# An encoder step on one core: the first attention block's query preparation moved ahead of the last gates, into shared ring buffers

## The chip, the cores and the metric

The kernel runs on one core of a Trainium2 chip. The metric is device time in microseconds (us) of one execution. Engines are named as the profile names them: PE (TensorE matmuls) with PEld (its weight loads), DVE (VectorE), ACT (ScalarE), POOL (GpSimd) and SP (SyncE, whose queue issues the DMAs).

## The reference, cut to what matters

One layer of a streaming encoder for 1024 prompt tokens and 64 sample tokens, width 1024, all in float32. One projection of the normalised input gives the columns of three branches and three gate blocks:

```
h = rmsnorm(x)
qa, ka, va, qi, ki, wi, ub, qm, gates = split(h @ w_in)
a = top-k sparse attention (8 query heads, 2 kv heads, head_dim 64)
b = causal pooling mixer of ub
m = cross-attention (4 heads, head_dim 128) into 256 memory tokens
mixed = sigmoid(ga)*(a @ w_oa) + sigmoid(gb)*(b @ w_ob) + sigmoid(gm)*(m @ w_om)
x = x + mixed @ w_out;  x = x + SwiGLU(rmsnorm(x))
```

Here only the gates `ga`, the memory branch `m`, its output product with `w_om` and the start of the attention branch `a` matter.

## The kernel before, in words

Every float32 product is made of three passes on halves: a value is split into a rounded high part and a low remainder, and `matmul3` (L117 to L124) issues high times high, high times low and low times high. A split costs one copy on ACT or POOL (`round_hi`) and one subtraction on DVE (`lo_of`, L88).

The code is written in one order, and a planner orders each engine's instructions when the program is built: an instruction that stands earlier in the code goes first among those that are ready, and one that stands later may be put into the gaps. What is fixed then is each engine's list; on the chip every engine works through its list in order and waits at each entry for its semaphores. `tc.issue_after(x)` puts the instructions of its block behind `x` in the list of `x`'s engine. A tile is a piece of a pool; tiles with one tag share the few buffers of this tag (`bufs`), each new tile taking a buffer that an older one has given back.

The part of the program that matters, in code order:

- The projections of the attention's queries, keys and values, nine token blocks each (L560 to L625). A key block is normalised, rotated, split (`kd`, L592 and L593), transposed on PE (L599), copied (`kt`, L602) and stored (`k_t`, L603).
- Gate blocks as fillers: `fill_gate(8, ...)` and `fill_gate(16, ...)`, then `fill_ob()`, the pooling branch's output product.
- The memory branch (L717 to L853), two halves of two heads each, in each half eight blocks of 128 tokens in a pipeline: queries transposed (L761), split (`qh`, `ql`), six logit products, softmax (maximum on DVE L727, exponential on ACT L732, scaling on POOL L735), transposes of the probabilities (L741), split (`ph`, `pl`), and for each pair of blocks twelve products with the values (L806, which the profile shows as L124 `mm<-ph,vh` and its like). Its result is split into `bh`, `bl`. Beside the blocks each half computes the 64 sample tokens (`sample`). The branch's key and value tiles are of tag `raw` (3 buffers): in each half `kc`, `vc`, and in step 1 of `sample` another `kc`, `vc` and the copy `kct` (L817).
- `fill_gate(0, side_a[:, 0], 0, 8)` (L857): the eight gate blocks of branch a. A block f loads its weights into `fraw`, splits them into one buffer of tag `whi` (POOL, L98) and one of `wlo` (DVE, L88), both tags with 2 buffers, and makes three chunks of 24 products each (`fl<-hh,whi` and its like), 576 products in all; ACT takes a tanh of each chunk (L247), SP stores it (L635). Code order puts them behind the memory branch; in time they fill its gaps.
- One `fill_om` (the memory branch's output product, 12 products), the load of the attention's first keys `kT`, then the first attention block's queries: `q0` (tag `raw`) is loaded (L877), split into `qs0` (L870 on ACT, L871 on DVE), transposed in eight pieces (L883) and copied to `qT0` (L884). `qs0` and `qT0` are tiles of a small pool `early` that lies on memory of the memory branch.
- The attention over query blocks. Its PSUM pool takes the banks of the pool before, and its SBUF pool takes the memory of the normalised input and of the gate tiles. Three `fill_om` come first, then the first block's logits (L1053); `split_values` (L1014, L1015) halves the values between the first softmax and the second.

Of the kernel before, what the change touches and what calls it, by code (L numbers as in the profile page):

```python
# [17 lines left out]
KT = D // 128  # L18
# [29 lines left out]
def encoder_step(ctx: ExitStack, tc: tile.TileContext, a: dict, o: list):  # L48
# [69 lines left out]
    def matmul3(ps, pairs, low_last=False):  # L118
        prods = [[(lh, rh), (lh, rl), (ll, rh)] for lh, ll, rh, rl in pairs]
        if low_last:  # L120
            prods = [[q for p in prods for q in p[:2]], [p[2] for p in prods]]
        prods = [q for p in prods for q in p]
        for i, (l, r) in enumerate(prods):
            PE.matmul(ps, l, r, start=i == 0, stop=i == len(prods) - 1)  # L124

    def rstd(r, ss, inv):
        G.tensor_scalar(r, ss, inv, EPS, op0=OP.mult, op1=OP.add)
# [81 lines left out]
    def raw_tile():  # L209
        return wp.tile([128, 1024], F32, name="raw", tag="raw", bufs=3)  # L210
# [32 lines left out]
    def fsig(w, c0, cn, low_last=False):  # L243
        ps = fps(cn)
        gate_block(w, hh[:, :, c0:c0 + cn], hl[:, :, c0:c0 + cn], ps, low_last)
        sg = fil.tile([128, 384], F32, name="fsg", tag="fsg", bufs=FSG + FPT)[:, :cn]
        A.activation(sg, ps, AF.Tanh, scale=0.5)  # L247
        return sg
# [379 lines left out]

    def fill_gate(base, dst, f0=0, f1=KT):
        for f in range(f0, f1):
            w = fgate(base + f)
            for c0, cn in CH:
                SP.dma_start(dst[f, :, c0:c0 + cn], fsig(w, c0, cn))  # L635

    def prepared(i):
        ts = split_tiles()
# [76 lines left out]
    fill_ob()  # L715

    MS = 128 ** -0.5  # L717
    if True:
        moh, mol = bh, bl
        gp_c = tc.tile_pool(name="gp", bufs=1)  # L720
        gp = gp_c.__enter__()
        with tc.tile_pool(name="matw", bufs=1) as mp:
# [41 lines left out]
            for half in range(2):  # L764
                hs2 = slice(2 * half, 2 * half + 2)
                pt, vc = mem_tiles(mem_k, mem_v, half)
                kh = mp.tile([128, 512], F32R, name="kh", tag="kh", bufs=1)
                kl = mp.tile([128, 512], F32R, name="kl", tag="kl", bufs=1)
                A.copy(kh, pt)
                lo_of(kl, pt, kh)  # L770
                vh = mp.tile([128, 2, 256], F32R, name="vh", tag="vh", bufs=1)
                vl = mp.tile([128, 2, 256], F32R, name="vl", tag="vl", bufs=1)
                A.copy(vh, vc)
                lo_of(vl, vc, vh)
                def query_of(t):
                    ps = queries(t * 128, 128, half)
                    qh = mp.tile([128, 256], F32R, name="qh", tag="qh", bufs=2)
                    ql = mp.tile([128, 256], F32R, name="ql", tag="ql", bufs=2)
                    A.activation(qh, ps, AF.Copy, scale=gqm_c)
                    V.scalar_tensor_tensor(ql, ps, gqm_c, qh.bitcast(F32), op0=OP.mult, op1=OP.subtract)  # L780
                    return qh, ql

                def probs_of(qh, ql):
                    lg = mm()
                    for h in range(2):
                        hs = slice(h * 128, (h + 1) * 128)
                        ms = slice(h * 256, (h + 1) * 256)
                        matmul3(lg[:, ms], [(qh[:, hs], ql[:, hs], kh[:, ms], kl[:, ms])])
                    return mem_softmax(lg, 128)

                def values_of(t, ex, pp_):
                    i = t % 2
                    if i == 0:
                        pp_[:] = [mp.tile([128, 4, 256], F32R, name="ph", tag="ph", bufs=1),
                                  mp.tile([128, 4, 256], F32R, name="pl", tag="pl", bufs=1)]
                    ph, pl = pp_
                    js = slice(i * 128, (i + 1) * 128)
                    pt = probs_t(ex, 128)
                    A.copy(ph[:, :, js], pt)
                    lo_of(pl[:, :, js], pt, ph[:, :, js])  # L800
                    if i == 0:
                        return
                    ps = mm()
                    for h in range(2):
                        hs = slice(h * 128, (h + 1) * 128)
                        matmul3(ps[:, h * 256:(h + 1) * 256],  # L806
                                [(vh[:, i, hs], vl[:, i, hs], ph[:, h * 2 + i], pl[:, h * 2 + i]) for i in range(2)])
                    pv = ps.rearrange("p (h t) -> p h t", h=2)
                    ts = slice((t - 1) * 128, (t + 1) * 128)
                    A.copy(moh[:, hs2, ts], pv)  # L810
                    lo_of(mol[:, hs2, ts], pv, moh[:, hs2, ts])

                def sample(t):
                    if t == 1:
                        pt, vc = mem_tiles(a["cache_mem_k"], a["cache_mem_v"], half)
                        kct = raw_tile()[:, :512]
                        A.copy(kct, pt)  # L817
                        sm_[:] = [vc, kct]
                    if t == 2:
                        ps = queries(SEQ, 64, half)  # L820
                        qs = mp.tile([128, 128], F32, name="qss", tag="qss", bufs=1)
                        A.activation(qs, ps, AF.Copy, scale=gqm_c)
                        sm_.append(qs)
                    if t == 4:
                        lg = mm()
                        for h in range(2):
                            PE.matmul(lg[:64, h * 256:(h + 1) * 256], sm_[2][:, h * 64:(h + 1) * 64],
                                      sm_[1][:, h * 256:(h + 1) * 256], start=True, stop=True)
                        sm_.append(mem_softmax(lg, 64))
                    if t == 6:  # L830
                        pt = probs_t(sm_[3], 64)
                        pT = mp.tile([128, 256], F32, name="pTs", tag="qn", bufs=2).rearrange("p (j t) -> p j t", j=4)
                        A.copy(pT, pt)
                        sm_.append(pT)
                    if t == 7:
                        ps = mm()[:, :128]
                        for h in range(2):
                            for i in range(2):
                                PE.matmul(ps[:, h * 64:(h + 1) * 64], sm_[0][:, i, h * 128:(h + 1) * 128],
                                          sm_[4][:, h * 2 + i], start=i == 0, stop=i == 1)  # L840
                        pv = ps.rearrange("p (h t) -> p h t", h=2)
                        A.copy(moh[:, hs2, SEQ:], pv)
                        lo_of(mol[:, hs2, SEQ:], pv, moh[:, hs2, SEQ:])

                qs_, exs, pp_, sm_ = {}, {}, [], []
                for t in range(11):
                    if t < 8:
                        qs_[t] = query_of(t)
                    if 0 <= t - 1 < 8:
                        exs[t - 1] = probs_of(*qs_[t - 1])  # L850
                    if 0 <= t - 3 < 8:
                        values_of(t - 3, exs[t - 3], pp_)
                    sample(t)  # L853


    rest = [(f, ci) for f in range(KT) for ci in (1, 0)]
    fill_gate(0, side_a[:, 0], 0, 8)  # L857
    for _ in range(1):
        fill_om(*rest.pop(0))
    kv_c = tc.tile_pool(name="kvp", bufs=1)  # L860
# [3 lines left out]
        SP.dma_start(kT[:, :, :, c0:c1].bitcast(F32), k_t[:, :, :, c0:c1])  # L864

    load_keys(0, 384)


    def split_queries(qs, q, n, eng=V):
        A.copy(qs[:n, :, 0], q[:n])  # L870
        eng.tensor_tensor(qs[:n, :, 1], q[:n], qs[:n, :, 0].bitcast(F32), op=OP.subtract)  # L871

    early_c = tc.tile_pool(name="early", bufs=1)
    early = early_c.__enter__()
    qT_first = early.tile([128, HA, 128], F32R, name="qT0")
    q0 = raw_tile()[:, :512].rearrange("p (h d) -> p h d", h=HA)
    SP.dma_start(q0.rearrange("p h d -> p (h d)"), q_a[TS[BLOCKS[0]][0]:TS[BLOCKS[0]][0] + 128])  # L877
    qs0 = early.tile([128, HA, 2, HDA], F32R, name="qs0")
    split_queries(qs0, q0, 128)
    for g in (0, 4):  # L880
        ps = mm(F32R)
        for h in range(4):
            PE.transpose(ps[:, h * 128:h * 128 + 128], qs0[:, g + h].rearrange("p s d -> p (s d)"), ident_r)  # L883
        A.copy(qT_first[:, g:g + 4], ps.rearrange("p (h t) -> p h t", h=4))  # L884


    for b in range(2):
# [112 lines left out]
    with tc.tile_pool(name="att", bufs=1, side="right") as ap_:  # L1000
# [130 lines left out]
        for b in BLOCKS:  # L1131
            qT = queries_t(b)
            for kv in range(2):
                probs = softmax(b, kv, qT)
                if not todo:
                    split_values()
                elif not a_held:
                    early_c.__exit__(None, None, None)
                    held_c = tc.tile_pool(name="held", bufs=1)
                    a_held.append(held_c.__enter__().tile([128, 4, 128 * len(HELD) - 64], F32, name="a_held"))  # L1140
                if todo:
# [574 lines left out]
```

## Time and profile before

| what | us |
| --- | --- |
| median of 3 runs (lowest to highest) | 1708.93 (1707.88 to 1710.14) |
| the profiled execution's own time | 1706.33 |
| its span in the trace | 1704.6 |
| PE busy (share of the span) | 1678.4 (98%) |
| DVE, ACT, POOL busy | 1136.4, 808.3, 410.2 |

Busy PE time counts the tail of each pipelined matmul, so where PE works without a break, the start of one product to the start of the next is the better measure. The table of stretches gives for each stretch its length, then for each engine the busy time and in brackets the number of instructions, then the granted clock of PE as a share of full speed, the DMA share and GB/s. In the timeline a row has start, duration, engine, line, operation, output and inputs, the count, and in square brackets the idle time of that engine before it with what ended it.

### The profile page before, as it was taken

The numbers are of one execution on the slowest core, as the hardware profiler recorded it, in microseconds if no ns is written. First come the engines' busy times: TensorE is split into PE (matmuls) and PEld (weight loads), VectorE is DVE, ScalarE is ACT, GpSimd is POOL, SyncE is SP. The second block draws the span as 40 slices with busy tenths as digits, with TensorE's granted clock in tenths as the row PEclk, the third lists the DMA queues.
The fourth block names the chain that finished last, engine by engine and source line by source line (L and its number), as shares of the span: only waits on it lengthen the run. The fifth ranks groups of instructions, "written<-read, shape, count | busy, mean of one in ns | idle before, by whom it ended". The sixth has DMA issues, their size and how long they took to land.

```text
span 1704.6 us, 32578 instructions
## 1 busy us (share of the span) xinstructions
PE 1678.4 (98%) x12037; PEld 1635.4 (96%) x12037; DVE 1136.4 (67%) x2552; ACT 808.3 (47%) x1942; POOL 410.2 (24%) x480
## 2 busy tenths in 40 slices
PE   9999999999999997999999999999999999999999
PEld 8999999999999997889898999999999999999999
DVE  7578999999973433767673676667657565575543
ACT  5456667755723444776532443334334333353331
POOL 4212424434431223553403431111111000000000
PEclk9999999999999999999999999999999999999999
DMA  6455851234365237435677634554535443596761
GB/s 226 135 181 204 280 158 47 73 129 146 118 217 162 87 102 243 127 119 170 215 266 257 196 117 133 195 195 149 188 113 182 146 170 103 177 368 220 213 189 54
DMA packets 158383, 288.61 MB, mean 169 GB/s; under 512 B 18184, under 2 KB 95872, under 8 KB 158224
## 3 DMA queue, kind: packets, MB, share of 16 engines
q1 hardware_dynamic: 158224, 286.53, 50.6%
q8 instruction: 95, 1.56, 0.4%
q14 instruction: 64, 0.52, 0.1%
HBM read 194.60 MB, written 91.87 MB: 168 GB/s over the span
## 4 chain that ended last, share of the span: by engine, by line
PE 55%; DVE 1%; ACT 1%; issue 0%; POOL 0%; DVEq 0%; ACTq 0%
PE mm L1370 25%; PE mm L1597 14%; PE mm L124 11%; PE fl L124 2%; PE acc L1093 1%; PE tr L1053 1%; PE mm L1085 1%; DVE pl L88 0%; POOL pr L1071 0%; ACT pr L1067 0%; ACT ph L1089 0%; PE mm L1308 0%; DVE pr L1065 0%; PE tr L124 0%; PE tr L1031 0%
## 5 line engine op out<-in xcount | busy, mean ns | idle before, releaser
L1370 PE MATMUL mm<-hi,whi 128*128 128x288 f32 (+1 forms) x1120 | 322.9, 289 | 1.1 <-ACT whi L1362 1.1
L1370 PE MATMUL mm<-lo,whi 128*128 128x288 f32 (+1 forms) x1120 | 323.4, 289 | 0.0
L1370 PE MATMUL mm<-hi,wlo 128*128 128x288 f32 (+1 forms) x1120 | 323.3, 290 | 0.0
L1370 PEld LDWEIGHTS mm<-hi,whi 128*128 128x128 f32 x1120 | 211.8, 189 | 1.6 <-ACT whi L1362 1.6
L1370 PEld LDWEIGHTS mm<-lo,whi 128*128 128x128 f32 x1120 | 211.7, 189 | 0.0
L1370 PEld LDWEIGHTS mm<-hi,wlo 128*128 128x128 f32 x1120 | 211.0, 189 | 0.0
L124 PE MATMUL fl<-hh,whi 128*128 128x362 f32 (+1 forms) x528 | 174.5, 330 | 0.0
L124 PE MATMUL fl<-hl,whi 128*128 128x362 f32 (+1 forms) x528 | 174.3, 330 | 0.0
L124 PE MATMUL fl<-hh,wlo 128*128 128x362 f32 (+1 forms) x528 | 173.8, 329 | 0.0
L1597 PE MATMUL mm<-ul,wh 128*128 128x256 f32 (+1 forms) x600 | 171.7, 288 | 0.0
L1597 PE MATMUL mm<-uh,wh 128*128 128x256 f32 (+1 forms) x600 | 171.1, 288 | 0.0
L1597 PE MATMUL mm<-uh,wl 128*128 128x256 f32 (+1 forms) x600 | 170.3, 288 | 0.0
L921 ACT ACTIVATE junk_a<-score,cand_a,sgn_a 128x512 f16<-128x512 f32 (+2 forms) x93 | 95.5, 1027 | 45.8 <-DVE cand_a L938 21.1
L1597 PEld LDWEIGHTS mm<-ul,wh 128*128 128x128 f32 x600 | 112.7, 188 | 0.0
L1597 PEld LDWEIGHTS mm<-uh,wh 128*128 128x128 f32 x600 | 112.4, 188 | 0.0
L1597 PEld LDWEIGHTS mm<-uh,wl 128*128 128x128 f32 x600 | 112.2, 188 | 0.0
L124 PEld LDWEIGHTS fl<-hh,whi 128*128 128x128 f32 x528 | 99.3, 188 | 0.7
L124 PEld LDWEIGHTS fl<-hh,wlo 128*128 128x128 f32 x528 | 99.3, 188 | 0.6
L124 PEld LDWEIGHTS fl<-hl,whi 128*128 128x128 f32 x528 | 99.3, 188 | 0.4
L88 DVE TENSOR_TENSOR wl<-raw,wh 128x512 fp32r<-128x512 f32 x75 | 51.8, 690 | 70.6 <-ACT wh L1587 70.5
L924 DVE TENSOR_SCALAR_CACHE_REDUCE junk_v<-score,cand_v 64x192 f16<-64x192 f32 (+1 forms) x124 | 93.9, 757 | 2.6
L1587 ACT CAST wh<-raw 128x512 fp32r<-128x512 f32 x75 | 46.6, 621 | 101.1 <-PE mm L1597 97.8
(447 smaller groups left out, 4638.3 us busy)
## 6 DMA issues: line engine op xcount, KB each, us to landing
uf<-u SPq DMA_DIRECT2D x75, 272.0 KB, 4.1
raw<-in_w_up_dram SPq DMA_DIRECT2D x26, 512.0 KB, 3.9
fraw<-in_w_gates_dram SPq DMA_DIRECT2D x23, 512.0 KB, 4.1
fr<-in_w_gate_dram SPq DMA_DIRECT2D x22, 512.0 KB, 4.0
dr<-in_w_down_dram SPq DMA_DIRECT2D x22, 512.0 KB, 6.0
s<-dr SPq DMA_DIRECT2D x22, 512.0 KB, 2.9
raw<-s SPq DMA_DIRECT2D x44, 256.0 KB, 4.0
whi<-w_pre SPq DMA_DIRECT2D x20, 512.0 KB, 4.0
```

Of the source, the lines that this page charges most:

```text
L88: return V.tensor_tensor(lo, src, hi.bitcast(F32), op=OP.subtract)
L124: PE.matmul(ps, l, r, start=i == 0, stop=i == len(prods) - 1)
L921: A.activation(junk[:n, :nk], sc, AF.Sign, bias=bj, scale=1.0 if scale is None else scale[:n, j:j + 1], accum_out=sj)
L924: V.tensor_scalar(junk[:n, :nk], sc, bj, None, op0=OP.is_ge, op1=OP.add, accum_out=sj)
L1053: lm = PE.matmul(lg[:n, i * 512:i * 512 + cn], qT[:, h, :n], kT[:, kv, s, k0 + c:k0 + c + cn], start=s == 0, stop=s == 1)
L1085: t_ = PE.transpose(pt[:cn, i * n:(i + 1) * n], probs[i][:, c:c + cn], ident[:n, :n])
L1093: m_ = PE.matmul(acc, vv, r, start=ji == 0 and i == 0, stop=ji == nj - 1 and i == 1)
L1370: PE.matmul(dst[i], l, r, start=start and j == 0, stop=stop and j == 11, skip_group_check=True)
L1587: A.copy(wh, raw)
L1597: PE.matmul(acc[f, i], l[:, fs], r[:, cs], start=start and j == 0, stop=stop and j == 2, skip_group_check=True)
```

## The change

Four edits.

1. The first block's queries move from behind `fill_gate(0, ...)` and the first `fill_om` to ahead of them, directly behind the memory branch. The pool `early` goes. `qT0` becomes a tile of tag `raw`, `qs0` a tile of tag `whi`; `q0` was and is of tag `raw`.
2. `matmul3` returns its last instruction, and `mem_mm[0]` keeps that of the memory branch's last value product. In the last of the eight gate blocks the second and third chunk (2 x 24 = 48 products) are put behind it on PE.
3. `qt_copy` keeps the last copy into `qT0`; `split_values` is put behind it on ACT.
4. The exit of pool `early` ahead of the tile `a_held` goes.

```
-    def fill_gate(base, dst, f0=0, f1=KT):
+    def fill_gate(base, dst, f0=0, f1=KT, last=None):
         for f in range(f0, f1):
             w = fgate(base + f)
             for c0, cn in CH:
-                SP.dma_start(dst[f, :, c0:c0 + cn], fsig(w, c0, cn))
+                with tc.issue_after(last) if last and f == f1 - 1 and c0 else nullcontext():
+                    sg = fsig(w, c0, cn)
+                SP.dma_start(dst[f, :, c0:c0 + cn], sg)
...
-                        matmul3(ps[:, h * 256:(h + 1) * 256],
-                                [(vh[:, i, hs], vl[:, i, hs], ph[:, h * 2 + i], pl[:, h * 2 + i]) for i in range(2)])
+                        mem_mm[:] = [matmul3(ps[:, h * 256:(h + 1) * 256],
+                                             [(vh[:, i, hs], vl[:, i, hs], ph[:, h * 2 + i], pl[:, h * 2 + i])
+                                              for i in range(2)])]
...
-    rest = [(f, ci) for f in range(KT) for ci in (1, 0)]
-    fill_gate(0, side_a[:, 0], 0, 8)
-    for _ in range(1):
-        fill_om(*rest.pop(0))
...
-    load_keys(0, 384)
...
-    early_c = tc.tile_pool(name="early", bufs=1)
-    early = early_c.__enter__()
-    qT_first = early.tile([128, HA, 128], F32R, name="qT0")
+    qT_first = wp.tile([128, 1024], F32R, name="qT0", tag="raw", bufs=3).rearrange("p (h t) -> p h t", h=HA)
     q0 = raw_tile()[:, :512].rearrange("p (h d) -> p h d", h=HA)
     SP.dma_start(q0.rearrange("p h d -> p (h d)"), q_a[TS[BLOCKS[0]][0]:TS[BLOCKS[0]][0] + 128])
-    qs0 = early.tile([128, HA, 2, HDA], F32R, name="qs0")
+    qs0 = wl.tile([128, 1024], F32R, name="qs0", tag="whi", bufs=2).rearrange("p (h s d) -> p h s d", h=HA, s=2)
     split_queries(qs0, q0, 128)
     for g in (0, 4):
...
-        A.copy(qT_first[:, g:g + 4], ps.rearrange("p (h t) -> p h t", h=4))
+        qt_copy = A.copy(qT_first[:, g:g + 4], ps.rearrange("p (h t) -> p h t", h=4)).ins
+
+    rest = [(f, ci) for f in range(KT) for ci in (1, 0)]
+    fill_gate(0, side_a[:, 0], 0, 8, mem_mm[0])
+    for _ in range(1):
+        fill_om(*rest.pop(0))
...
+    load_keys(0, 384)
...
                 if not todo:
-                    split_values()
+                    with tc.issue_after(qt_copy):
+                        split_values()
                 elif not a_held:
-                    early_c.__exit__(None, None, None)
                     held_c = tc.tile_pool(name="held", bufs=1)
```

More of the change, by code (lines that the diff above doesn't have):

```diff
@@ L123, in matmul3 @@
         for i, (l, r) in enumerate(prods):
-            PE.matmul(ps, l, r, start=i == 0, stop=i == len(prods) - 1)
+            m_ = PE.matmul(ps, l, r, start=i == 0, stop=i == len(prods) - 1)
+        return m_.ins
     def rstd(r, ss, inv):
@@ L717, in encoder_step @@
     MS = 128 ** -0.5
+    mem_mm = []
     if True:
@@ L853, in encoder_step, with split_queries @@
                     sample(t)
+    def split_queries(qs, q, n, eng=V):
+        A.copy(qs[:n, :, 0], q[:n])
+        eng.tensor_tensor(qs[:n, :, 1], q[:n], qs[:n, :, 0].bitcast(F32), op=OP.subtract)
+    qT_first = wp.tile([128, 1024], F32R, name="qT0", tag="raw", bufs=3).rearrange("p (h t) -> p h t", h=HA)
+    q0 = raw_tile()[:, :512].rearrange("p (h d) -> p h d", h=HA)
+    SP.dma_start(q0.rearrange("p h d -> p (h d)"), q_a[TS[BLOCKS[0]][0]:TS[BLOCKS[0]][0] + 128])
+    qs0 = wl.tile([128, 1024], F32R, name="qs0", tag="whi", bufs=2).rearrange("p (h s d) -> p h s d", h=HA, s=2)
+    split_queries(qs0, q0, 128)
+    for g in (0, 4):
+        ps = mm(F32R)
+        for h in range(4):
+            PE.transpose(ps[:, h * 128:h * 128 + 128], qs0[:, g + h].rearrange("p s d -> p (s d)"), ident_r)
+        qt_copy = A.copy(qT_first[:, g:g + 4], ps.rearrange("p (h t) -> p h t", h=4)).ins
     rest = [(f, ci) for f in range(KT) for ci in (1, 0)]
-    fill_gate(0, side_a[:, 0], 0, 8)
+    fill_gate(0, side_a[:, 0], 0, 8, mem_mm[0])
     for _ in range(1):
@@ L866, in encoder_step @@
     load_keys(0, 384)
-    def split_queries(qs, q, n, eng=V):
-        A.copy(qs[:n, :, 0], q[:n])
-        eng.tensor_tensor(qs[:n, :, 1], q[:n], qs[:n, :, 0].bitcast(F32), op=OP.subtract)
-    early_c = tc.tile_pool(name="early", bufs=1)
-    early = early_c.__enter__()
-    qT_first = early.tile([128, HA, 128], F32R, name="qT0")
-    q0 = raw_tile()[:, :512].rearrange("p (h d) -> p h d", h=HA)
-    SP.dma_start(q0.rearrange("p h d -> p (h d)"), q_a[TS[BLOCKS[0]][0]:TS[BLOCKS[0]][0] + 128])
-    qs0 = early.tile([128, HA, 2, HDA], F32R, name="qs0")
[L879 to L884, printed above, removed]
     for b in range(2):
```

## The prediction

> **What bounds the kernel now.** I read the page, then the table of stretches between the end of the projections and the first attention logits, then the timeline of each stretch. The page:
>
> ```profile
> span 1704.6 us, 32578 instructions
> PE 1678.4 (98%) x12037; PEld 1635.4 (96%) x12037; DVE 1136.4 (67%) x2552; ACT 808.3 (47%) x1942; POOL 410.2 (24%) x480
> ```
>
> PE is the bound nearly everywhere: whatever leaves PE without work is paid, whatever another engine does beside it is free. The profiled execution took 1706.33 us, 1.73 us more than its span and 2.60 below the median of the runs (1708.93). I work out a difference on the profiled one and add it to the median. About 0.2% (3.4 us) is what a measurement of this kernel can tell from no change.
>
> The stretches around the change, the last row from a later stage for the clock:
>
> ```profile
> 495.20:540.40 45.20, 45.20 (x321) 44.61 (x320) 17.02 (x46) 14.80 (x49) 8.61 (x15) 1.00 0.56 168
> 540.40:602.30 61.90, 61.90 (x424) 60.42 (x424) 27.40 (x59) 28.45 (x82) 13.31 (x23) 1.00 0.35 108
> 602.30:652.45 50.15, 50.06 (x337) 48.29 (x335) 18.38 (x41) 19.55 (x56) 10.66 (x19) 1.00 0.32 102
> 652.45:659.57 7.12, 0.85 (x9) 0.74 (x9) 1.29 (x2) 4.49 (x13) 3.07 (x6) 0.84 0.90 285
> 840.00:844.00 4.00, 2.85 (x19) 2.06 (x18) 2.46 (x5) 2.80 (x6) 0.22 (x1) 1.00 0.71 264
> ```
>
> PE is full through the key projection and the memory branch (three rows), then nearly empty for 7.12 us. The timeline of that hole:
>
> ```profile
> 652.17 0.28 PE L124 MATMUL mm<-ph,vl 128*128 128x256 f32 x1
> 654.53 0.85 PE L883 MATMUL mm<-ident_r,qs 128*128 128x128 f32 x8 [2.09 <-DVE qs L871]
> 659.57 0.69 PE L124 MATMUL fl<-bh,whi 128*128 128x384 f32 x1 [4.18 <-ACT qT L884]
> 663.89 0.43 PE L124 MATMUL mm<-bl,whi 128*128 128x384 f32 x1
> 667.80 0.33 PE L124 MATMUL mm<-bh,wlo 128*128 128x384 f32 x1
> ```
>
> The branch's last value product, the query transposes after a wait for their split, the first output product after a wait for the copy `qT`. Behind the hole the clock is low: from 659.57 to 663.89 thirteen steps take 0.33 us each, from there to 667.80 twenty-two take 0.18; 13 x 0.16 = 2.1 us. The hole costs 7.12 + 2.1 = 9.2 us, of which 0.85 are the transposes themselves. That is what the change can win.
>
> What fills PE up to 652.45? The gate blocks of branch a. The same stretches for instructions on `fl` alone, and the first and last of 37 gate products in a row:
>
> ```profile
> 495.20:540.40 45.20, 28.30 (x164) 26.76 (x162) 1.05 (x2) 2.85 (x6) 1.00 0.56 168
> 540.40:602.30 61.90, 42.70 (x234) 38.38 (x234) 0.00 (x0) 4.77 (x10) 1.00 0.35 108
> 602.30:652.45 50.15, 35.13 (x195) 31.69 (x193) 0.56 (x1) 3.81 (x8) 1.00 0.32 102
> 630.88 0.33 PE L124 MATMUL fl<-hh,wlo 128*128 128x364 f32 x1
> 636.87 0.33 PE L124 MATMUL fl<-hh,wlo 128*128 128x362 f32 x1
> ```
>
> 36 steps in 5.99 us are 0.166 us a product. So 162 gate products (27 us) lie in the first stretch, 233 (39 us; one of 234 is cut off at each edge) in the second, 181 (30 us, beside 12 of `fill_om`) in the third: 576, 96 us, all of them ahead of the hole, and 66 us of them ahead of 602.30.
>
> **The change, part by part.** *The move into ring tiles.* `qs0` takes a buffer of tag `whi`, and in the code it now stands ahead of all eight gate blocks, whose high halves are of that tag. Are buffers of one tag given to whoever is ready, or in code order? The ring `raw` answers:
>
> ```profile
> 533.62 0.68 DVE L88 TENSOR_TENSOR vl<-raw,vh 128x512 fp32r<-128x512 f32 x1
> 539.79 0.33 SPq L113 DMA_DIRECT2D fraw<-in_w_gates_dram  x1
> 541.72 0.37 SPq L747 DMA_DIRECT2D raw<-mem_k  x1
> 541.72 0.59 ACT L817 COPY raw<-mm 128x512 f32<-128x512 f32 x1 [3.68 <-PE mm L753]
> 599.31 0.32 SPq L877 DMA_DIRECT2D raw<-q_a  x1
> ```
>
> The second half's keys (`raw<-mem_k`) were in DRAM long before. From 534.30 (533.62 + 0.68) the buffer of the first half's values was free and SP went on issuing other loads (539.79). The keys went out only at 541.72, with the copy `kct` (L817), which stands ahead of them in the code. So a later tile waits until every earlier one of its tag has its buffer. By that rule no gate block of branch a can have its `whi` before `qs0` has its own, that is before `q0` has landed; and `q0` stands behind all the branch's `raw` tiles and was loaded at 599.31, in step 1 of the second half. Before, nobody waited for that load. Now 395 gate products that ran ahead of 602.30 can't.
>
> *First stretch, 495.20 to 540.40, without its 27 us of gates.* What then ends PE's waits is the key chain:
>
> ```profile
> 502.87 0.43 DVE L593 TENSOR_TENSOR kd<-qr,kd 128x256 fp32r<-128x256 f32 x1 [0.47 <-ACT kd L592]
> 506.04 0.22 PE L599 MATMUL mm<-ident_r,kd 128*128 128x128 f32 x1
> 513.82 0.43 DVE L593 TENSOR_TENSOR kd<-qr,kd 128x256 fp32r<-128x256 f32 x1 [0.91 <-ACT kd L592]
> 516.87 0.22 PE L599 MATMUL mm<-ident_r,kd 128*128 128x128 f32 x1
> 520.24 0.22 ACT L216 ACTIVATE hjunk<-mm 64x64 f32<-64x64 f32 x1 [2.08 <-PE mm L124]
> 523.99 1.08 DVE L593 TENSOR_TENSOR kd<-qr,kd 64x256 fp32r<-64x256 f32 x1 [0.47 <-ACT kd L592]
> 528.42 0.37 ACT L602 CAST kt<-mm 128x256 fp32r<-128x256 f32 x1 [4.08 <-PE mm L599]
> 532.18 0.80 SPq L758 DMA_DIRECT2D qn<-q_m  x2
> k_t<-kt SPq DMA_DIRECT2D x9, 256.0 KB, 3.4
> qn<-q_m SPq DMA_DIRECT2D x16, 128.0 KB, 2.3
> ```
>
> The transposes at 506.04 and 516.87 had their input at 503.30 and 514.25: 2.7 and 2.6 us come back. From the last projection (520.24) to the branch's first logits (540.40, the edge of the stretch) there is a chain: `kd` ready 4.8 us later (525.07), transposes and `kt` 0.9, the store's landing 3.4, which gives the branch its memory, the query load 2.3, and its transposes, copy, subtraction and hand-offs about 2 (estimate): 13.4 in place of 20.2, another 6.8 back. The stretch shrinks by 12.1 while 27.0 of work leave it: PE idles 14.9 us more.
>
> *Second stretch, 540.40 to 602.30.* Without gates 61.9 - 38.8 = 23.1 us of PE work stay. How fast does the branch run alone? The steps of one block's chain, late in the second half:
>
> ```profile
> 637.68 0.48 ACT L779 ACTIVATE qh<-mm,gqm_c 128x256 fp32r<-128x256 f32 x1 [2.46 <-PE mm L761]
> 638.59 0.68 DVE L727 TENSOR_REDUCE mx<-mm 128x2 f32<-128x512 f32 x1
> 641.24 0.94 POOL L735 TENSOR_SCALAR ex<-ex,sm 128x256 f32<-128x256 f32 x2 [9.28 <-PE fl L124]
> 642.48 0.59 ACT L799 CAST ph<-mm 128x512 fp32r<-128x512 f32 x1 [0.76 <-PE mm L741]
> 643.10 0.69 DVE L88 TENSOR_TENSOR pl<-mm,ph 128x512 fp32r<-128x512 f32 x1 [0.16 <-ACT ph L799]
> ```
>
> Copy 0.48 and a subtraction like it, maximum to scaling 2.65 (638.59 to 641.24), scaling 0.94, copy 0.59, subtraction 0.69: 5.8 us off PE. With PE's part (23.1 us over some ten blocks, 2.3) a block's chain is about 8.1 us. The exponentials and the queries have two buffers, the pair `ph`, `pl` one: two blocks overlap, so about 4 us a block. The floor is the busiest engine: ACT's 28.45 less ten tanh (4.77) is 23.7, or 2.4 a block; the ceiling is today's 61.9. I take 4.0, near the chain, because two buffers let no more than two run: ten blocks, 40 us. PE idles 40 - 23.1 = 16.9 us.
>
> *The halved ring.* `qs0` keeps its `whi` until its transposes, and their PSUM tiles stand in the code behind the branch's last. So until the branch ends the gates have one buffer: each block's split waits for the block before. A copy plus its hand-offs is some 1.4 us (estimate, from copies like POOL's 0.94 above), once for the first block and about twice more until the branch ends: 4.2 us, less what of the branch fits in; bounds 0 and 4.2.
>
> *Behind that* the remaining branch and all 576 products run densely, as from 602.30 to 652.45, and PE ends with gates. The branch is done tens of us earlier, so the 48 tied products wait for nothing and cost 0; the hole of 7.12 us goes with its slow clock, and the transposes' 0.85 lie within full PE. Were the tie to bind, it would hold behind it on PE the output products and first logits, and through tanh and store the release of the gate tiles' memory, which the attention's loads of values and queries and its first reductions wait for.
>
> *Edits at nothing.* `split_values` behind `qt_copy` on ACT: the copy is long done; without that cover the copies of values wait 1 us at most. The third `obx` load waits for `qT0`'s buffer until the first block's logits; its readers come in the attention's second half. The vanished pool `early` frees SBUF that nobody waits for. On SP, `q0` goes out at its turn as before; the key load follows the branch.
>
> Sum: 14.9 + 16.9 + 4.2 = 36.0 us of new idle time, less 7.12 - 0.85 = 6.3 and 2.1 for the clock: +27.6 us. 1706.33 becomes 1733.9, the median 1736.5.
>
> A row and a rule on the clock: PE was busy with loads for only 2.06 of 4.00 us at 840 to 844, and the granted clock stayed 1.00; by that row the thinned branch keeps its clock. The Trainium skill, "TensorE: Matmul & The Clock Gate", section "A second HAM failure mode: psum-queue depth-cycling", says that short idle times between groups of matmuls that cycle through PSUM banks can make the clock swing between half and full. By it the sum would lie above mine (second rival).
>
> **Rivals.** *Faster: buffers go to whoever is ready.* Place: the `whi` ring at about 611, where one falls free while `q0` waits. If `qs0` may come late there, the gates keep filling and only the hole goes. Price: -9.2 + 0.85, and back about 2 us (estimate) because 48 products, 8 us, leave the tail of the branch, whose own chain then shows: -6.4, so 1702.5. It decides if a gate of branch a is seen ahead of `q0`'s load. Against it: 541.72 above. For it: only that a single place shows the rule. 0.08.
>
> *Slower still: half clock in the thinned branch.* After a wait of 4.18 us the clock was halved at once; the first stretch will hold one longer. If it stays low, PE's 23.1 us in the second stretch double, and since half of a chain's steps lie beside another block's, some 16 us show: 1752.5. Against it the row at 840. 0.12.
>
> *No difference.* The branch alone runs at its floor (23.7, so 0.6 of idle time), the ring costs 0, the first stretch 10: +2.2, 1711.1. It needs perfect overlap of four engines working in order. 0.04, of it 0.03 within 0.2%.
>
> **How the numbers follow.** My forecast has 0.76: 1736.5. Its own bounds: 3.0 to 4.8 us a block moves it by -10 and +8, the first stretch by 3, the ring by -4: 1720 to 1748. The range reaches up to the half clock and leaves the faster rival and the floor out: 1719 to 1753. Faster by over 0.2%: 0.08. Within: 0.03. Slower: 0.76 + 0.12 + 0.01 = 0.89.
>
> **What would show it.** Right: no gate product of branch a ahead of the load `raw<-q_a`; PE holes of 1 to 3 us from 495 to about 570 with some 32 us of idle time in sum, the largest (about 11 us) ahead of the branch's first logits; the query load near 565; gates dense until about 685; no hole ahead of the first logits. Wrong: gates among the key projection as now, a branch that still ends near 650, or a hole that stays ahead of the first output product.

## The result, and the profile after

The changed kernel takes 1733.15 us (median of 4 runs, 1731.88 to 1733.58) against 1708.41 us before (4 runs, 1706.42 to 1710.14): 1.0144 times as long, 95% interval 1.0126 to 1.0162, or 24.7 us more. The forecast was 1736.5, +27.6.

The page of the changed kernel, its first two lines. The profiled execution took 1733.58 us.

```profile
span 1731.7 us, 32597 instructions
PE 1686.1 (97%) x12037; PEld 1638.5 (95%) x12037; DVE 1135.2 (66%) x2552; ACT 809.2 (47%) x1942; POOL 407.8 (24%) x480
```

The span grew by 27.1 us, PE's busy time by only 7.7: most of the loss is PE with nothing to do. The table of stretches shows where. Its edges are the events that the forecast named: the first logits of the memory branch (527.97), the first gate product of branch a (568.88), the end of the branch (614.05), the last gate product (685.02), the attention's first logits (694.32). The columns are those of the prediction's table: PE, PEld, DVE, ACT, POOL, granted clock, DMA share, GB/s.

```profile
495.20:527.97 32.77, 21.70 (x167) 20.03 (x166) 12.23 (x44) 12.16 (x44) 5.29 (x11) 0.85 0.46 134
527.97:568.88 40.91, 30.98 (x198) 27.03 (x199) 23.82 (x58) 23.38 (x68) 9.39 (x19) 0.83 0.31 99
568.88:614.05 45.17, 42.83 (x294) 40.81 (x293) 20.55 (x44) 21.08 (x62) 11.83 (x20) 1.00 0.21 63
614.05:685.02 70.97, 70.97 (x429) 70.97 (x427) 6.82 (x6) 8.66 (x18) 5.22 (x5) 1.00 0.35 119
685.02:694.32 9.30, 8.56 (x49) 8.27 (x49) 1.66 (x3) 0.47 (x1) 3.04 (x3) 1.00 0.71 223
```

Before, PE was busy for 45.20 of 45.20 and 61.90 of 61.90 us in the first two stretches; now it stands partly empty in both, at a reduced clock, and then runs gates alone for 71 us. The same on the timeline:

```profile
519.04 0.31 PE L600 MATMUL mm<-ident_r,kd 64*128 64x64 f32 x1 [3.11 <-ACT kd L593]
...
526.74 1.09 PE L765 MATMUL mm<-ident,qn 128*128 128x128 f32 x4 [5.85 <-DMA qn<-q_m]
...
566.04 0.42 SPq L867 DMA_DIRECT2D raw<-q_a  x1
...
568.88 0.33 PE L124 MATMUL fl<-hh,whi 128*128 128x364 f32 x1
...
613.94 0.28 PE L124 MATMUL mm<-ph,vl 128*128 128x256 f32 x1
614.05 0.33 PE L124 MATMUL fl<-hh,wlo 128*128 128x364 f32 x1
...
685.02 0.34 PE L124 MATMUL fl<-bh,whi 128*128 128x384 f32 x1
...
688.00 0.41 PE L124 MATMUL fl<-bh,whi 128*128 128x384 f32 x1 [0.74 <-DVE gt L698]
...
694.32 0.85 PE L1055 MATMUL tr<-kT,qT 128*128 128x384 f32 x4
```

No gate product of branch a lies ahead of the load `raw<-q_a`; before, the first ran at 495.2. The two long waits are the key chain that the gates used to cover: 3.11 us for the last keys' split and 5.85 us for the branch's first queries. The load of `q0` came at 566.04 (forecast: near 565), gates ended at 685.02 (forecast: about 685), and the hole of 7.12 us ahead of the first output products is gone: at 685.02 there is no wait.

### The profile page after: what moved, and what is told of

The parts are those of the page before. It is cut to its first block, busy times and chain, and to the rows that moved or that the text cites. A ratio compares the mean times of both kernels' runs of the same rounds, so it can differ in the third digit from the quotient of the medians.

```text
span 1731.7 us, 32597 instructions
## 1 busy us (share of the span) xinstructions
PE 1686.1 (97%) x12037; PEld 1638.5 (95%) x12037; DVE 1135.2 (66%) x2552; ACT 809.2 (47%) x1942; POOL 407.8 (24%) x480
## 4 chain that ended last, share of the span: by engine, by line
PE 55%; DVE 1%; ACT 1%; issue 0%; POOL 0%; DMA 0%; DVEq 0%; ACTq 0%
PE mm L1372 25%; PE mm L1599 13%; PE mm L124 10%; PE fl L124 2%; PE acc L1095 1%; PE mm L1087 1%; PE tr L1055 1%; DVE pl L88 0%; PE tr L124 0%; DMA wlo<-wlo_d 0%; POOL pr L1073 0%; ACT pr L1069 0%; ACT ph L1091 0%; PE mm L1310 0%; DVE pr L1067 0%
```

## The experiments

Three theories were set against each other. A: `qs0` stands ahead of the gate blocks in the order of the ring `whi`, so the gates get their place in the engines' queues behind `q0`'s load. B: with `qs0` in it the ring has too few buffers, whatever the order. C: the tie, and what stands behind it, holds up the attention. In the diffs - is the changed kernel (for `tie_only`, the kernel before). Ratios are against the kernel before, run on the same chip.

**The tie taken out (`no_tie`).**

```diff
-    fill_gate(0, side_a[:, 0], 0, 8, mem_mm[0])
+    fill_gate(0, side_a[:, 0], 0, 8)
```

> The changed kernel without the tie of the last 48 gate products. Theory A, the order of the ring (qs0 stands ahead of the gate blocks in the code, so they follow q0's load): the tie binds nothing, because in the changed kernel the memory branch ended at 614.05 and the tied products ran long behind it; 1733 us, within 2, first gate product again near 569 us. Rival B, shortage (with qs0 in it the ring has one whi buffer for the gates, whatever the order): the same, 1733. Rival C, the tie (the tied products and what stands behind them on TensorE, through tanh and store, hold up the attention): most of the 25 us come back, about 1710.

1733.14 us, ratio 1.0146 (1.0131 to 1.0162). The first gate product came at 565.91, again behind everything in the first stretch. C falls: the tie costs nothing here, since the branch ends 71 us before the gates do.

**The query block back in its old place (`late_ring`).** Ring tiles and tie stay.

```diff
-    qT_first = wp.tile(... tag="raw", bufs=3) ... qt_copy = A.copy(...)
     rest = [(f, ci) for f in range(KT) for ci in (1, 0)]
     fill_gate(0, side_a[:, 0], 0, 8, mem_mm[0])
...
     load_keys(0, 384)
+    qT_first = wp.tile(... tag="raw", bufs=3) ... qt_copy = A.copy(...)
```

> The changed kernel with the query block moved back behind the gate blocks, the first output block and the key load, where it stood before; ring tiles and tie are kept. Theory A: the gates have their buffers first and run from about 495 us again; the 48 tied products fill most of the hole ahead of the first logits, at the cost of 2 to 3 us of the branch's own chain in its last blocks: about 1702, between 1700 and 1706. Rival B (shortage): the ring is whole until the queries come, so the same. Rival C (the tie costs): slower than before, 1715 or more. A fourth possibility, that any use of ring tiles for the queries costs: about 1709, the hole as before, since the split of the queries would wait for the last gate block.

1706.17 us, ratio 0.9988 (0.9979 to 0.9997). All of the 25 us are gone and 2 more. So the place in the code makes the loss, not the use of ring tiles. The time lies 0.2 us above the range that was expected (1700 to 1706); `tie_only`, below, asks where the rest went.

**The halved queries out of the ring `whi` (`own_qs`).** The place in the code and the tie stay.

```diff
-    qs0 = wl.tile([128, 1024], F32R, name="qs0", tag="whi", bufs=2)...
-    split_queries(qs0, q0, 128)
     for g in (0, 4):
+        qs0 = gp.tile([128, 2, 384], F32R, name="gt", tag="gt", bufs=4)...[:, :512]...
+        split_queries(qs0, q0[:, g:g + 4], 128)
```

> The changed kernel with the halved queries in two tiles of the ring gt of the merge (unused until the first output products) and not in whi; place in the code, qT0 in the ring raw and the tie are kept; the split is made in two halves. Theory A: no gate block stands behind the queries, gates run from about 495 us, q0 is loaded near 600, the transposes come inside the branch, no hole ahead of the first logits: 1699 to 1704. Rival B: the same. Rival C: slower than before, 1715 or more. A fourth possibility, that qT0 in the ring raw (one buffer less for the loads) is what costs: stays near 1733.

1703.46 us, ratio 0.9972 (0.9962 to 0.9981). The table of stretches for instructions on `fl` alone, one row each of `no_tie`, `late_ring` and `own_qs`, with PE and PEld first:

```profile
495.20:540.40 45.20, 0.23 (x2) 0.00 (x0) 1.02 (x2) 0.00 (x0) 0.81 0.47 140
```

```profile
495.20:540.40 45.20, 28.16 (x162) 26.48 (x160) 0.79 (x2) 2.85 (x6) 1.00 0.56 168
```

```profile
495.20:540.40 45.20, 28.30 (x164) 26.92 (x163) 1.08 (x2) 2.84 (x6) 1.00 0.46 137
```

Before, it was 28.30 us in 164 products. Either way of letting the gates go first (a later place, another ring) brings all of them back into the key projection, with the clock at 1.00 in place of 0.81. `qT0` in the ring `raw` is not what costs.

**Order or shortage: `q0` loaded early (`q0_own`).** Only the load's tile is changed; `qs0` still takes one of two `whi` buffers ahead of all gates and keeps it to the branch's end.

```diff
-    q0 = raw_tile()[:, :512]...
+    q0 = gp.tile([128, 2, 384], F32, name="gt", tag="gt", bufs=4)...[:, :512]...
```

> The changed kernel with the query load q0 alone in a tile of the ring gt, so that it need not wait for the branch's raw tiles; qs0 stays in whi, ahead of the gates, and holds one of the two buffers through the whole branch. This tells order from shortage. Theory A: the gates start as soon as q0 is there, which is when the key projection's memory is free, near 528 us, and then fill the branch with one buffer; the first stretch keeps its 14.6 us of idle time, the second loses its 16.7 but for some 4 us of waits for the single buffer: about 1720, between 1714 and 1723. Rival B (shortage): one buffer stays one buffer, 1730 or more. Rival C: near 1733.

1717.53 us, ratio 1.0056 (1.0042 to 1.0069): 15.6 of the 24.7 us came back. Its timeline, and its table of stretches from the first gate product to the last:

```profile
515.05 1.04 POOL L98 TENSOR_SCALAR whi<-fraw 128x1024 fp32r<-128x1024 f32 x1
...
522.64 0.54 SPq L867 DMA_DIRECT2D gt<-q_a  x1
...
528.19 0.36 PE L124 MATMUL fl<-hh,whi 128*128 128x364 f32 x1
```

```profile
528.19:665.94 137.75, 136.72 (x907) 133.11 (x907) 48.62 (x104) 51.69 (x144) 24.00 (x43) 1.00 0.33 105
```

The load moved 43.4 us ahead (566.04 to 522.64), and the first gate product moved with it, 40.7 us (568.88 to 528.19). From there PE idled at most 1.0 of 137.75 us although the gates had a single buffer until 628 us, and the branch's last product ran at 631. So shortage (B) costs 1 us at the most; the order (A), by which the gates come behind the load, costs the rest. The first stretch still has no gates, and its loss stays (32.99 us against 32.77).

**The tie alone, on the kernel before (`tie_only`).**

```diff
-    fill_gate(0, side_a[:, 0], 0, 8)
+    fill_gate(0, side_a[:, 0], 0, 8, mem_mm[0])
```

> The kernel before with the tie of the last 48 gate products alone; queries in their own memory behind the branch. In the changed kernel with the query block moved back, first logits came 4.3 us earlier than before and the time was 1706.2. Theory A (ring tiles as such cost nothing, only the place in the code does): this kernel differs from that one by the ring tiles alone and gives 1705 to 1707.5. Rival: the ring tiles cost by themselves: this kernel is 1703 or less.

1703.12 us, ratio 0.9972 (0.9962 to 0.9983). A missed by 2 us, and the rival's 1703 was not quite reached: with the same order of code and without the ring tiles this kernel was 3 us faster than `late_ring`. The two intervals overlap a little. Nor do the two differ by the ring tiles alone: `late_ring` also keeps `split_values` behind `qt_copy`, and this one does not. So whether the ring tiles cost anything stays open. The loss lies behind `late_ring`'s first logits, which come earlier than here (663.63 against 666.13): its profile has a wait of 2.13 us for `pr` in the first softmax of the attention that this one has not, and POOL came to `pr` at 671.93 only, behind the halving of values and queries.

**Own memory, no tie (`own_qs_no_tie`), and half the tie (`own_qs_24`).** The edits are the first diff above on `own_qs`, and

```diff
-            for c0, cn in CH:
-                with tc.issue_after(last) if last and f == f1 - 1 and c0 else nullcontext():
+            for ci, (c0, cn) in enumerate(CH):
+                with tc.issue_after(last) if last and f == f1 - 1 and ci == 2 else nullcontext():
```

> The changed kernel with the queries' halves in the ring gt (1703.5 us) and without the tie. Theory A: the transposes still come before the branch's end, so of the old hole only the split of the branch's last output stays, some 2 us, and the branch's tail keeps its 48 fillers: 1701 to 1704. Rival (the tie is what fills the hole): the hole of 7 us with its low clock is back, 1706 to 1709.

> As the changed kernel with the queries' halves in the ring gt, but with only the last 24 gate products tied (the third chunk of the last block). The tied 48 took 8.0 us where some 2.1 us were to be covered, and the branch's tail, without its fillers, lost about 3 us. With 24 tied, 4.0 us stand behind the branch and 24 products go back into the tail: 1.5 us off 1703.5, 1701 to 1703.

Without a tie: 1701.83 us, ratio 0.9963 (0.9950 to 0.9975), the lowest median here, about 6 us below the kernel before and 31 below the changed one; its interval overlaps those of `own_qs` and `tie_only`. Half the tie: 1706.78, ratio 0.9995 (0.9985 to 1.0004), a miss by 4 us. Timelines of `own_qs_no_tie`, then of `own_qs_24`:

```profile
651.38 0.37 SPq L1008 DMA_DIRECT2D vf<-v_a  x1
...
652.38 0.28 PE L124 MATMUL mm<-ph,vl 128*128 128x256 f32 x1
654.05 0.44 PE L124 MATMUL fl<-bh,whi 128*128 128x384 f32 x1 [1.40 <-DVE bl L88]
...
660.74 0.97 PE L1055 MATMUL tr<-kT,qT 128*128 128x384 f32 x4 [0.17 <-DMA kT<-k_t]
```

```profile
649.60 0.28 PE L124 MATMUL mm<-ph,vl 128*128 128x256 f32 x1
...
661.77 0.37 SPq L1008 DMA_DIRECT2D vf<-v_a  x1
...
663.04 0.85 PE L1055 MATMUL tr<-kT,qT 128*128 128x384 f32 x4
...
668.64 0.56 DVE L698 SCALAR_TENSOR_TENSOR gt<-gt,fl 128x384 f32<-128x384 f32 x1 [4.38 <-DMA gt<-side_m]
...
669.73 0.62 PE L1055 MATMUL tr<-kT,qT 128*128 128x384 f32 x2 [3.41 <-DVE mx L1067]
```

Without the tie little stays of the hole: 1.40 us for the split of the branch's last output (`bl`) and 0.17 for the keys; transposed queries were waiting. With half the tie the first logits came no earlier than with the whole (663.04 and 663.12): the 24 products that were freed ran between 635.25 and 641.75, ahead of the branch's last value products and not in the gaps there (1.8 us of waits for `ph` in both kernels), so the branch ended 3.9 us later (its last product 649.60 against 645.71) and 24 products behind it fewer, 4.0 us, made up for just that. And a tied gate has followers: the attention's value load (`vf`) went out at 661.77, 1.3 us ahead of the first logits, where it had 3.5 us with the whole tie (659.62), 9.4 without a tie and 16.3 before (651.67 and 667.97). Why half the tie sends it out later than the whole one was not taken apart. A merge load behind `vf` on SP then kept DVE for 4.38 us and the second logits for 3.41.

**What paces the thinned branch (`warm`, `deep_ex`, `deep_ph`).** `warm` adds 64 products that nothing reads, ahead of the query block:

```diff
+    for g in range(4):
+        ps = fps(364)
+        with tc.issue_after(mem_tr[0]):
+            for k in range(16):
+                PE.matmul(ps, ident_r, hh[:, k % 8, :364], start=k == 0, stop=k == 15)
```

> The changed kernel with 64 added products of the identity with columns of hh (10.7 us of TensorE, in four PSUM tiles that nothing reads) tied behind the first transposes of the memory branch, so that they fall into the idle time ahead of the branch's first logits. They keep TensorE busy there, and so tell whether the half clock from 515 to 543 us costs time. Chain theory (two blocks in flight set the pace of the thinned branch): the products vanish in idle time, the clock is full, and the time stays at 1731 to 1734. Clock theory: of the 6.8 us by which the thinned branch's products were longer most comes back, 1726 to 1728. If the added products cost their own time: 1738 or more.

1739.19 us, ratio 1.0181 (1.0167 to 1.0194): they cost time of their own, since they stood ahead of the branch's first query transposes on PE and pushed these from 526.74 to 530.88. The question still has part of an answer, in the rows from the first query transposes to the first gate product, of the changed kernel and of `warm`:

```profile
526.74:568.88 42.14, 32.07 (x202) 27.72 (x203) 23.84 (x58) 23.91 (x69) 9.39 (x19) 0.82 0.33 106
```

```profile
530.88:573.01 42.13, 31.72 (x208) 28.02 (x206) 23.85 (x57) 23.81 (x69) 9.40 (x19) 0.88 0.29 92
```

The granted clock went from 0.82 to 0.88, the time stayed 42.1. Read as time at half clock (twice the missing share), that is 15.2 us against 10.1. So 5 us of half clock less, 2.5 us of work at most, bought nothing to be seen, though some of the added products still lie in the row. `no_tie` has the same 202 products from its first query transposes (524.95) to its first gate product (565.91): 40.96 us at 0.87. By that pair 4.5 us of half clock less go with 1.2 us less time. So the half clock costs little here; that the other 10 us of it are as cheap was not tried.

`deep_ex` puts the exponentials in the ring `gt` (four buffers for two) and gives the scaled queries three; `deep_ph` has those exponentials, two pairs of `ph`, `pl` (the diff shows `ph`) and two tanh tiles less.

```diff
-                ex = mp.tile([128, 2, 256], F32, name="ex", tag="ex", bufs=2)[:n]
+                ex = gp.tile([128, 2, 384], F32, name="gt", tag="gt", bufs=4)...[:n]
```

```diff
-                        pp_[:] = [mp.tile([128, 4, 256], F32R, name="ph", tag="ph", bufs=1),
+                        pp_[:] = [mp.tile([128, 4, 256], F32R, name="ph", tag="ph", bufs=2),
```

> The changed kernel with deeper buffers for the exponentials (four, in the ring gt) and the scaled queries (three). It asks what sets the pace of the branch while it has no gates to fill it: from its first logits to the first gate product it took 40.9 us in the changed kernel. If it is the two buffers of exponentials and queries, as the prediction put it, the stretch shrinks by 5 us or more and the time goes to about 1728. If it is the single pair of ph and pl, or the chain itself with the order of the engines' queues, the stretch stays within 2 us of 40.9 and the time at 1731 to 1734.

> The changed kernel with two pairs of ph and pl in place of one, the exponentials in the ring gt (four), and for the memory of that two tiles less for the gates' tanh (three in place of five). If the single pair ph, pl sets the pace of the thinned branch, its stretch shrinks by 5 us or more against 40.9. If the chain and the order of the queues do, it stays within 2 us. The tanh tiles can cost time in other stages, so that the stretch decides and not the whole time.

1728.96 us (1.0120, 1.0105 to 1.0135) and 1729.06 (1.0119, 1.0102 to 1.0136). From the branch's first logits to the first gate product:

```profile
526.58:563.12 36.54, 29.46 (x198) 25.36 (x199) 23.65 (x58) 23.62 (x70) 9.40 (x19) 0.92 0.27 80
```

```profile
528.00:563.82 35.82, 29.85 (x199) 26.44 (x199) 23.24 (x58) 23.33 (x68) 9.39 (x19) 0.88 0.28 81
```

40.91 became 36.54 and 35.82. More exponentials and queries in flight bring 4.4 us, between the two outcomes expected. `deep_ph` brings 5.1, which is what was expected if the pair `ph`, `pl` set the pace; but it has the deeper exponentials too, and against `deep_ex` (which has the third query buffer that `deep_ph` has not) the pair adds 0.7 us. So buffers are a part of the pace. Some 12 of the 16.8 us that the stretch was longer than its work are left, and no run takes them apart: in `deep_ex` PE still waits 7.1 us, 3.0 of them for `ph` and 2.8 for query loads.

## Why the prediction was right

Point by point, in lost time, which is waits and slower products together. The two profiles stand 1.6 us apart before the change acts: at 495.20 the changed kernel still had nine output products of the earlier stage to do (the last at 496.6), which no step of the change touches.

- *The first stretch*: forecast 14.9 us of idle time. Measured 32.77 less 18.2 of work (45.20 less 27.0 of gates) less those 1.6: 13.0. The branch's first logits came at 527.97, 12.4 us earlier than before, or 14.0 with the 1.6 taken off; the forecast had 12.1.
- *The second stretch, 4.0 us a block*: forecast 16.9. Its 198 products other than gates took before 23.1 us for 190, so 24.1 of work; 40.91 - 24.1 = 16.8. That it fits so closely is in part luck. PE waited only 40.91 - 30.98 = 9.9 us of it, and the other 6.9 are products that took longer, at a clock of 0.83 that the forecast had not counted. And half of the waits end with the landing of a query load, a step that the forecast's chain of 8.1 us left out:

```profile
PE mm L765 <- DMA qn<-q_m: 5.1, 4, 2.3
PE mm L124 <- ACT ph L803: 4.8, 4, 1.6
```

  Nor do two buffers alone set the 4.0 us a block, as the forecast had it: with four for the exponentials and three for the queries `deep_ex` still takes 36.54 us.
- *The halved ring*: forecast 4.2 with bounds 0 and 4.2. Between 568.88 and 614.05 lie 150 gate products (25.0), the transposes (0.75) and the rest of the branch (16.9): 45.17 - 42.65 = 2.5 us idle, of which `q0_own` leaves at most 1.0 to the ring. This term was mis-sized.
- *The hole and its clock*: forecast -6.3 and -2.1. Both came: no wait at 685.02, and the clock in the last row is 1.00, where it had been 0.84 in the hole and 0.73 from there to the first logits.
- *Not forecast*: 0.9 us between 685.02 and 694.32, a second output block that waits 0.74 for DVE's product with the first, where before the first twelve lay inside the branch and were done long ahead.

13.0 + 16.8 + 2.5 + 0.9 - 8.4 = 24.8 at the first logits, and with the 1.6 of before 26.4: 694.32 less 667.97 is 26.35. Some 0.8 more is lost in the attention (27.1 by the spans); `split_values` behind `qt_copy` has no run of its own. The medians, which do not hang on this one pair of executions, say 24.7.

One sign came out otherwise. The forecast saw some 32 us of idle time from 495 to about 570, with a hole of about 11 us ahead of the branch's first logits. PE stood idle for 21.0 us there (11.1 and 9.9), and the longest hole was 5.85 us; the rest of the lost time is slower products and the 1.6 us.

*The rule of the ring* carried the forecast, and its effect is shown by four kernels: gates from 495 us when `qs0` follows them or is not in their ring, from 528 when `q0` is there at 522.64, from 569 when it is there at 566.04. But the wording was too strong. "No gate block of branch a can have its `whi` before ... `q0` has landed" describes a wait, and the profile shows none. POOL in the changed kernel:

```profile
556.49 0.93 POOL L739 TENSOR_SCALAR ex<-ex,sm 128x256 f32<-128x256 f32 x2 [3.64 <-DVE sm L737]
557.89 0.93 POOL L739 TENSOR_SCALAR ex<-ex,sm 128x256 f32<-128x256 f32 x2 [0.47 <-DVE sm L737]
558.79 1.04 POOL L98 TENSOR_SCALAR whi<-fraw 128x1024 fp32r<-128x1024 f32 x1
```

The first gate block's rounding ran at 558.79, 7.3 us before `q0`'s load was issued, with no idle time ahead of it: it had waited for its turn behind the branch's scalings, which themselves waited for DVE. Nothing else is seen to hold it. The load of its weights went out at 331.30, the last products on the ring's older tiles were over by 497, and POOL stood empty for 15.56 us ahead of the scaling at 532.89; before the change the same rounding ran at 481.45. In `q0_own` it is the same (515.05, 7.6 us before the load). What the ring's order fixes is the place in each engine's queue. POOL then followed that order although the data of the later instruction had long been there.

*The rivals.* Faster (buffers to whoever is ready): fell with 568.88. No difference: the floor of 2.4 us a block was not reached, 4.1 was. Half clock: the condition came in for a part of the stretch, and the price of 16 us on top of the chain did not. In the changed kernel:

```profile
519.00:526.70 7.70, 1.85 (x8) 1.32 (x8) 1.71 (x3) 1.48 (x3) 0.00 (x0) 0.50 0.42 106
...
536.00:540.00 4.00, 4.00 (x20) 4.00 (x20) 2.02 (x5) 2.64 (x9) 0.93 (x2) 0.50 0.22 66
```

The clock was at half from 518 to about 542 us, through most of the first three blocks, and the branch kept its 4.1 us a block. The reading is that PE's slower products fell into time in which it would for the most part have waited; `warm` and `no_tie` bear that out for some 5 us of half clock, and the rest is argued. Behind 549 the clock stayed at 1.00 although PE went on waiting 1 to 2 us at a time. The rule of the Trainium skill that the prediction weighed ("TensorE: Matmul & The Clock Gate", "A second HAM failure mode: psum-queue depth-cycling") would let it swing there; this run does not show it, but two others do. In `warm` the clock had come back to 1.00 and fell again behind a wait of 1.64 us:

```profile
554.00:557.00 3.00, 3.00 (x16) 3.00 (x16) 1.48 (x4) 1.35 (x5) 0.93 (x2) 0.50 0.12 38
```

In `deep_ex` it was 0.50 over 562 to 564, behind a wait of 1.51 us. So the row at 840 did not carry over, and that the clock held in the changed kernel behind 549 is no rule.

*The tie* was costed at nothing, and `no_tie` shows nothing (1733.14 and 1733.15). What the prediction said it would hold if it were to bind is what `own_qs_24` shows: the value load, and first reductions that wait for a load behind it.

## What to carry to other kernels

A tile that shares a ring with filler work should stand in the code where its data arrives, not where it is wanted early: here 4 KB a partition that waited for one late load sent 426 products, 71 us of filler, behind the stage that they were to fill. Taking the tile from an idle ring cured it without moving anything else; moving the load earlier brought 15.6 of the 24.7 us back. And filler that is held back for a hole can leave one where it came from and delay what follows it: here, once the queries were ready early, no tie at all did at least as well as the whole one (1701.83 and 1703.46, with overlapping intervals) and better than half of it (1706.78).

## What the runs showed of the hardware that was not expected

Once low, the clock came back late: PE was busy without a wait from 535.91 to 541.26 us and the clock was still 0.50 over 536 to 540. "TensorE: Matmul & The Clock Gate" in the Trainium skill ("What's actually happening") gives about 3.4 us of sustained work for the return; here it took more than 4, though a part of that work is transposes, and no run shows whether they count like other products. It also fell early: of the wait of 3.11 us that ended at 519.04 the clock was 1.00 up to 517.5 and 0.50 from 518.0, some 2 us into it. In the hole of the kernel before, where PE's wait began at 655.4, it was 1.00 up to 657 and 0.50 from 658.
